# Strassen's seven products in the first product of two MLPs, with the first layer's second product over two tiles at a time

## The chip, the cores and the metric

The kernel runs on one core of a Trainium2 chip, as one program. Its time is the device time of one execution in microseconds (us); several runs are given by their median. Within a core, PE multiplies matrices, DVE and ACT work elementwise on SBUF and PSUM, POOL elementwise on SBUF alone, and SP issues the DMAs. Each engine works through a list of its own in order, and waits on semaphores for the others.

## The reference

A backbone of two layers over 256 context tokens and 512 latent tokens, 1024 features wide, in float32. The first layer has windowed attention, the second a two-way RWKV-7 scan; each is followed by the same MLP:

```python
def sq_relu_mlp(h, w1, w2):
    return jnp.square(jax.nn.relu(h @ w1)) @ w2
...
x = x + gt2 * sq_relu_mlp(rmsnorm(x, norm2_g[i]) * (1.0 + sc2) + sh2, mlp_w1[i], mlp_w2[i])
```

w1 is 1024 x 4096 and w2 4096 x 1024. The first layer's MLP runs over all 768 tokens (context with its own shift, scale and gate), the second's over the 512 latent ones. Attention and scan are not touched by the change.

## The kernel before

Activations lie transposed: a tile has 128 features on the partitions and the tokens along the free dimension, so X is 8 tiles of 128 x 768 (first layer) or 128 x 512 (second).

Every large product is made of three. A float32 value is split into `hi`, its value in the PE's faster float32 format (fp32r), and `lo`, the remainder; `mm3` (L357) then adds hi x hi, hi x lo and lo x hi into one PSUM bank, each as one matmul per 512 columns. So 768 columns take two matmuls, of 512 and of 256, for each of the three (`halves`, L372). `split` (L328) makes `hi` of a weight tile by a copy on ACT or POOL in turn and `lo` by a subtraction on DVE (L337). Activations are split the same way: `normed` (L304) multiplies X by the norm's factors (L313, tile `nu`), makes `hi` with the shift on ACT (L316) and `lo` on DVE (L317), and for every third tile on POOL (L325).

`mlp` (L664) has two steps. `w1(g)` makes four of the 32 hidden tiles: for each, `wtile` (L339) loads 128 x 1024 of w1 and splits it, `gemm` (L376) runs 8 feature tiles x `mm3`, ACT takes the relu from PSUM (L689) and its square as `hi` (L690), DVE the square again (L691) and the remainder (L692). `w2(g)` takes those four hidden tiles: for each of 8 output tiles m it loads 128 x 512 of w2 (L699), splits it (L703), runs 4 x `mm3` into a bank, and DVE adds the bank, times the gate, to X (`add_gated`, L657, two instructions of 256 and 512 columns in the first layer; L711, one, in the second). The loop calls w1(g), then w2(g-1), for 8 groups.

The framework orders the instructions of each engine: it takes what the program issues, places it by a timeline of its own estimates, and lets an instruction move ahead of others on its engine where its operands allow. `behind_norm` (L297) keeps what is issued under it behind two instructions of the norm (`norm_ins`). Buffers are handed out by pools with a number of copies per tag; an instruction that fills a copy waits for the last reader of what was in it. [...]

In front of each MLP stands its norm (`norm_stats` L263 in the first layer, the same steps at L1655 in the second): squares, sums over features by matmul, a square root on ACT, a reciprocal on DVE, a broadcast by matmul. The end of the first MLP computes the norm of the next layer the same way.

Of the kernel before, what the change touches and what calls it, by code (L numbers as in the profile page):

```python
# [166 lines left out]
HP = 0  # L167
MERGE = {True: 3, False: 1}


class K:
    def __init__(self, ctx, tc, a, stop=None, dbg=None):
# [121 lines left out]
            nc.scalar.activation(acc[:, sl], bc[:, 0:nt * P], AF.Copy)  # L294
        self.norm_ins = (act.ins, dve.ins)

    def behind_norm(self):  # L297

        st = ExitStack()
        for i in self.norm_ins:  # L300
            st.enter_context(self.tc.issue_after(i))
        return st

# [357 lines left out]
                                                ALU.mult, ALU.add)  # L661


    def mlp(self, l, bc):  # L664
# [12 lines left out]
        GF = 4
        hids = {}

        def w1(g):  # L680
            later = self.behind_norm() if g == 0 else ExitStack()
            hid = [mp.tile([P, GF, n], F32R, tag=f"hid{i}", bufs=2, name=f"hid{i}") for i in range(2)]
            for j in range(GF):
                ps = self.big("w1_ps")
# [4 lines left out]
                nc.scalar.activation(r, ps[:, 0:n], AF.Relu)  # L689
                nc.scalar.activation(hid[0][:, j], r, AF.Square)  # L690
                nc.vector.tensor_tensor(r, r, r, ALU.mult)  # L691
                nc.vector.tensor_tensor(hid[1][:, j], r, hid[0][:, j].bitcast(F32), ALU.subtract)  # L692
            hids[g] = hid

        def w2(g):
            hid = hids.pop(g)
            for m in range(8):
                raw = mp.tile([P, 512], F32, tag="w2raw", bufs=2, name="w2raw")
                nc.sync.dma_start(raw, a["w2"][l, g, m])  # L699
                wh = mp.tile([P, 512], F32R, tag="w2h", bufs=5, name="w2h")  # L700
                wl = mp.tile([P, 512], F32R, tag="w2l", bufs=5, name="w2l")
                with self.behind_norm() if g == 0 else ExitStack():
                    self.split(raw, wh, wl)  # L703
# [4 lines left out]
                if l == 0:
                    self.add_gated(ps, m, u0 + 5)
                else:  # L710
                    nc.vector.scalar_tensor_tensor(self.X[:, m], ps[:, 0:S], self.ada[:, u0 + 5, m, 0:1],  # L711
                                                   self.X[:, m], ALU.mult, ALU.add)
# [1065 lines left out]
```

## Time and profile before

| | |
|---|---|
| three runs, median (least to most) | 2259.94 us (2255.7 to 2265.13) |
| profiled execution, its own time | 2270.0 us |
| its span, first to last instruction | 2268.2 us |
| mean granted PE clock | 0.944 |
| PE busy | 2049.9 us, 90% of the span |
| DVE busy | 1320.1 us, 58% |
| ACT, POOL busy | 857.2 us, 38%; 263.7 us, 12% |
| DMA read and written | 191.80 MB and 32.60 MB |

Times are from the start of the span. A row of a timeline gives start, duration, engine, line, operation, output<-input, the shape, and in brackets how long the engine had been idle and who ended that. A grouped row gives count, busy time, mean duration in ns, and the idle time ahead of the group with its releasers. PEld is PE's loading of weights, which overlaps its matmuls. `w_ps` is the bank of either product of the MLP; `mhh` and `mhl` are hi and lo of the normed activations, `hid` those of the hidden tiles, `whi`, `wlo`, `w2h`, `w2l` those of the weights.

### The profile page before, as it was taken

The numbers are of one execution on the slowest core, as the hardware profiler recorded it, in microseconds if no ns is written. First come the engines' busy times: TensorE is split into PE (matmuls) and PEld (weight loads), VectorE is DVE, ScalarE is ACT, GpSimd is POOL, SyncE is SP. The second block draws the span as 40 slices with busy tenths as digits, with TensorE's granted clock in tenths as the row PEclk, the third lists the DMA queues.
The fourth block names the chain that finished last, engine by engine and source line by source line (L and its number), as shares of the span: only waits on it lengthen the run. The fifth ranks groups of instructions, "written<-read, shape, count | busy, mean of one in ns | idle before, by whom it ended". The sixth has DMA issues, their size and how long they took to land. (4 is left out here: it accounts for less than half of the span.)

```text
span 2268.2 us, 40460 instructions
## 1 busy us (share of the span) xinstructions
PE 2049.9 (90%) x16208; PEld 1668.3 (74%) x16208; DVE 1320.1 (58%) x2737; ACT 857.2 (38%) x1702; POOL 263.7 (12%) x362
## 2 busy tenths in 40 slices
PE   5989999979999999997979798698869887999999
PEld 4876756868888888885856687586658655787887
DVE  4465565464334343349787665888898657444443
ACT  4344454232111111116454445567647433222121
POOL 0122232010000000001010101000000101101110
PEclk9999999989999999997999898789889898999999
DMA  8344461122122121116146434113311312323322
GB/s 288 102 135 135 138 212 58 56 79 65 61 61 66 56 70 61 53 37 236 63 162 244 135 129 155 35 51 90 95 48 58 128 56 79 103 93 95 96 88 80
DMA packets 115885, 229.67 MB, mean 101 GB/s; under 512 B 12912, under 2 KB 31088, under 8 KB 115312
## 3 DMA queue, kind: packets, MB, share of 16 engines
q1 hardware_dynamic: 115696, 227.08, 31.1%
q8 instruction: 128, 2.10, 0.4%
q14 instruction: 61, 0.50, 0.1%
HBM read 191.80 MB, written 32.60 MB: 99 GB/s over the span
## 5 line engine op out<-in xcount | busy, mean ns | idle before, releaser
L337 DVE TENSOR_TENSOR wlo<-wraw,whi 128x1024 fp32r<-128x1024 f32 (+1 forms) x121 | 134.5, 1120 | 322.6 <-ACT whi L334 169.2
L364 PE MATMUL w_ps<-mhl,whi 128*128 128x512 f32 (+1 forms) x768 | 235.7, 361 | 7.3 <-DVE mhl L317 7.3
L362 PE MATMUL w_ps<-mhh,whi 128*128 128x512 f32 (+1 forms) x768 | 235.1, 361 | 7.1 <-POOL whi L336 3.4
L366 PE MATMUL w_ps<-mhh,wlo 128*128 128x512 f32 (+1 forms) x768 | 235.4, 361 | 5.0 <-DVE wlo L337 5.0
L364 PE MATMUL w_ps<-hid,w2h 128*128 128x512 f32 (+1 forms) x768 | 234.0, 359 | 0.0
L362 PE MATMUL w_ps<-hid,w2h 128*128 128x512 f32 (+1 forms) x768 | 231.4, 355 | 1.6 <-ACT mrelu L689 1.4
L366 PE MATMUL w_ps<-hid,w2l 128*128 128x512 f32 (+1 forms) x768 | 231.1, 355 | 0.0
L334 ACT ACTIVATE w2h<-w2raw 128x512 fp32r<-128x512 f32 x64 | 40.4, 631 | 330.0 <-PE w_ps L364 299.1
L660 DVE SCALAR_TENSOR_TENSOR X<-w_ps,ada,X 128x256 f32<-128x256 f32 (+1 forms) x128 | 73.1, 612 | 137.5 <-PE w_ps L366 137.5
L364 PEld LDWEIGHTS w_ps<-mhl,whi 128*128 128x128 f32 x768 | 127.7, 190 | 33.0 <-DVE mhl L317 9.8
L362 PEld LDWEIGHTS w_ps<-mhh,whi 128*128 128x128 f32 x768 | 127.8, 190 | 31.7 <-POOL whi L336 4.1
L366 PEld LDWEIGHTS w_ps<-mhh,wlo 128*128 128x128 f32 x768 | 127.8, 190 | 31.0 <-DVE wlo L337 8.0
L336 POOL TENSOR_SCALAR whi<-wraw 128x1024 fp32r<-128x1024 f32 (+1 forms) x60 | 69.2, 1154 | 673.2 <-PE w_ps L364 252.6
L366 PEld LDWEIGHTS w_ps<-hid,w2l 128*128 128x128 f32 x768 | 127.4, 189 | 23.3
L362 PEld LDWEIGHTS w_ps<-hid,w2h 128*128 128x128 f32 x768 | 125.5, 188 | 24.8 <-ACT mrelu L689 2.3
L334 ACT ACTIVATE whi<-wraw 128x1024 fp32r<-128x1024 f32 (+1 forms) x61 | 59.1, 968 | 222.7 <-PE w_ps L364 100.8
L364 PEld LDWEIGHTS w_ps<-hid,w2h 128*128 128x128 f32 x768 | 126.6, 188 | 20.7
L689 ACT ACTIVATE mrelu<-w_ps 128x768 f32<-128x768 f32 (+1 forms) x64 | 44.7, 699 | 189.6 <-PE w_ps L366 189.6
L1238 PE MATMUL g_ps<-pad,bk 128*128 128x128 f32 x640 | 98.1, 306 | 6.1 <-DVE gm L1244 2.1
L1238 PEld LDWEIGHTS g_ps<-pad,bk 128*128 128x128 f32 x640 | 86.0, 212 | 15.9 <-ACT pad L1235 7.5
L564 DVE CUSTOM_DVE_ANT_0 sm<-sc_ps,consts,vecs 128x256 f32<-128x256 f32 (+2 forms) x96 | 71.6, 760 | 40.7 <-PE pt_ps L585 21.9
L337 DVE TENSOR_TENSOR w2l<-w2raw,w2h 128x512 fp32r<-128x512 f32 x128 | 89.1, 697 | 4.8 <-ACT w2h L334 4.6
(381 smaller groups left out, 4486.1 us busy)
## 6 DMA issues: line engine op xcount, KB each, us to landing
ada_w<-ada_w SPq DMA_DIRECT2D x160, 256.0 KB, 3.5
wraw<-w SPq DMA_DIRECT2D x64, 512.0 KB, 3.2
w2raw<-w SPq DMA_DIRECT2D x128, 256.0 KB, 2.6
kt<-ada_w SPq DMA_DIRECT2D x32, 256.0 KB, 5.1
feat<-cs SPq DMA_DIRECT2D x16, 390.0 KB, 2.3
cs<-feat SPq DMA_DIRECT2D x24, 260.0 KB, 3.1
wraw<-wq SPq DMA_DIRECT2D x8, 512.0 KB, 3.8
wraw<-wo SPq DMA_DIRECT2D x8, 512.0 KB, 3.2
```

Of the source, the lines that this page charges most:

```text
L334: nc.scalar.activation(hi, raw, AF.Copy)
L336: nc.gpsimd.tensor_scalar(hi, raw, 1.0, 0.0, ALU.mult, ALU.add)
L337: nc.vector.tensor_tensor(lo, raw, hi.bitcast(F32), ALU.subtract)
L362: nc.tensor.matmul(o, wh, cut(xh, sl), start=start, stop=False)
L364: nc.tensor.matmul(o, wh, cut(xl, sl), start=False, stop=False)
L366: nc.tensor.matmul(o, wl, cut(xh, sl), start=False, stop=stop)
L564: nc.vector.tensor_tensor_reduce(sm[:, :nk], ps[:, :nk], self.c["band"][:, b0:b0 + nk], rs[:, h:h + 1], self.v["sink"][:, hd:hd + 1], ALU. ...
L660: self.nc.vector.scalar_tensor_tensor(self.X[:, m, sl], ps[:, sl], self.ada[:, u, m, s:s + 1], self.X[:, m, sl], ALU.mult, ALU.add)
L689: nc.scalar.activation(r, ps[:, 0:n], AF.Relu)
L1238: nc.tensor.matmul(g[:, P * k:P * k + P], it.BK[:, d, b + k], pv[:, :, k], start=True, stop=True)
```

## The change

The first product is computed for two hidden tiles at a time. The two tiles' weights and the activations are each cut into 2 x 2 blocks: weights by hidden tile and by half of the features (blocks of 128 x 512), activations by half of the features and half of the tokens (four tiles of 128 x H, with H 384 in the first layer and 256 in the second). Strassen's algorithm in Winograd's form needs seven block products in place of eight, and sums of blocks: four sums of activations, made once (`block_sums`), four of weights per pair, and seven additions of results. A block product is 4 feature tiles x three matmuls of H columns. The very first pair is computed plainly, from the four blocks in their original state, while the norm is still running; `block_sums` then overwrites them.

Seven split blocks of activations replace the eight tiles (`mbh`, `mbl`). In `pair`, of the seven weight remainders DVE makes four and POOL three; POOL also makes one sum of weights, and part of the block sums. ACT makes every `hi`. DVE adds the results from PSUM; relu and square become one instruction of DVE (L807). Weights of the first product are loaded into the MLP's own pool.

In the first layer GF, the number of hidden tiles that the second product sums in PSUM, goes from 4 to 2: there are 16 groups in place of 8, w2 tiles are 128 x 256, and `add_gated` runs twice as often. Every other remainder of w2 is made by POOL there. In the second layer GF stays 4.

The core of the diff:

```diff
+    def normed_w(self, u2, x, bc, gain, sh, l, n, bh, bl):
...
+        for k in range(NF):
+            u = u2[k % 4][:, k // 4]
+            hi, lo = ((t[:, 0:7:6, k % 4] if k < 4 else t[:, 1:3, k % 4]) for t in (bh, bl))
+            uh = u.rearrange("p (a h) -> p a h", a=2)
+            for s, t0, w in streams:
+                c = slice(t0, t0 + w)
+
+                with self.tc.issue_after(done[k - 2]) if k > 1 else ExitStack():
+                    nc.vector.scalar_tensor_tensor(u[:, c], x[k][:, c], gain[:, k, s:s + 1], bc[:, c], ALU.mult, ALU.mult)
+                if l == 0:
+                    nc.scalar.activation(u[:, c], u[:, c], AF.Identity, bias=sh[:, k, s:s + 1])
+            if l == 0:
+                act = nc.scalar.activation(hi, uh, AF.Copy)
+                dve = nc.vector.tensor_tensor(lo, uh, hi.bitcast(F32), ALU.subtract)
...
+    def block_sums(self, u2, H, bh, bl):
...
+        for k in range(4):
+            u0a, u0b, u1a, u1b = (u2[k][:, i, h * H:h * H + H] for i in range(2) for h in range(2))
+            nc.vector.tensor_tensor(u0b, u0b, u0a, ALU.subtract)
+            nc.vector.tensor_tensor(u1b, u1b, u0b, ALU.subtract)
+            ts.append((u1b, u0b, u0a, u1a))
+        for b, i in ((4, 0), (3, 1), (5, 2), (6, 3)):
+            for k in range(4):
+                t = ts[k][i]
+                if b == 5:
+                    nc.gpsimd.tensor_tensor(t, ts[k][0], t, ALU.subtract)
+                if b == 6:
+                    nc.gpsimd.tensor_tensor(t, t, ts[k][0], ALU.subtract)
+                act = nc.scalar.activation(bh[:, b, k], t, AF.Copy)
+                eng = nc.gpsimd if b == 6 else nc.vector
+                lo = eng.tensor_tensor(bl[:, b, k], t, bh[:, b, k].bitcast(F32), ALU.subtract)
...
     def mlp(self, l, bc):
...
+        n = T if l == 0 else S
+        H = n // 2
+        GF = 2 if l == 0 else 4
...
+        def first_pair():
...
+            for k in range(NF):
+                q = ((0, 6), (1, 2))[k // 4]
+                for ps, (wh, wl) in zip(banks, ws):
+                    for w, t, e in ((wh, bh, 0), (wh, bl, 1), (wl, bh, 2)):
+                        for h in range(2):
+                            nc.tensor.matmul(ps[:, 512 * h:512 * h + H], w[:, k * P:k * P + P], t[:, q[h], k % 4],
+                                             start=(k == 0 and e == 0), stop=(k == NF - 1 and e == 2))
+            with self.behind_norm():
+                self.block_sums(u2, H, bh, bl)
...
+        def pair(m, hid, j):
...
+            def product(tag, raw, b, eng=None):
+                bank = self.ps.tile([P, 512], F32, tag=tag, bufs=2 if tag == "t" else 1, name="w1p_ps")[:, 0:H]
+                wh, wl = block()
+                nc.scalar.activation(wh, raw, AF.Copy)
+                (eng or nc.vector).tensor_tensor(wl, raw, wh.bitcast(F32), ALU.subtract)
+                for k in range(4):
+                    self.mm3([(bank, slice(0, H))], wh[:, k * P:k * P + P], wl[:, k * P:k * P + P],
+                             bh[:, b, k], bl[:, b, k], k == 0, k == 3)
+                return bank
...
+            def square(i):
+                nc.vector.scalar_tensor_tensor(c[i], c[i], 0.0, c[i], ALU.max, ALU.mult)
+                nc.scalar.activation(hid[0][:, j + i], c[i], AF.Copy)
+                nc.vector.tensor_tensor(hid[1][:, j + i], c[i], hid[0][:, j + i].bitcast(F32), ALU.subtract)
+
+            nc.vector.tensor_tensor(s1, a21, a22, ALU.add)
+            nc.vector.tensor_tensor(s2, s1, a11, ALU.subtract)
+            nc.vector.tensor_tensor(s4, a12, s2, ALU.subtract)
+            nc.gpsimd.tensor_tensor(a21, a11, a21, ALU.subtract)
+            b, p1 = product("a", a11, 0), keep()
+            nc.scalar.activation(p1, b, AF.Copy)
+            add(c11, product("t", a12, 1, nc.gpsimd), p1)
+            p3 = product("t", s4, 2)
+            q = add(keep(), product("o", s2, 4), p1)
+            p5 = product("a", s1, 3)
+            w = add(keep(), p5, q)
+            add(c12, p3, w)
+            square(0)
+            z = add(keep(), product("t", a21, 5, nc.gpsimd), q)
+            add(c22, p5, z)
+            add(c21, product("o", a22, 6, nc.gpsimd), z)
+            square(1)
...
+        def w2(g):
...
+            W = P * GF
+            c0 = W * g % 512
+            for m in range(8):
+                raw = mp.tile([P, W], F32, tag="w2raw", bufs=2, name="w2raw")
...
+                with self.behind_norm(self.sums_ins) if g == 0 else ExitStack():
+                    nc.scalar.activation(wh, raw, AF.Copy)
+                    eng = nc.gpsimd if l == 0 and m % 2 else nc.vector
+                    eng.tensor_tensor(wl, raw, wh.bitcast(F32), ALU.subtract)
```

`keep` and the sums have buffers of their own; `add` is one DVE addition of a bank and a kept tile. The split weights rotate in four half tiles in the first layer and six in the second.

More of the change, by code (lines that the diff above doesn't have):

```diff
@@ L168 @@
 MERGE = {True: 3, False: 1}
+WL = (0, 1)
+NSQ = 3
+NRW = (2, 3)
 class K:
@@ new lines, in mlp, with block, keep, add @@
+    def mlp(self, l, bc):
+        if l not in WL:
+            return self.mlp_plain(l, bc)
+        nc, a = self.nc, self.a
+        st = ExitStack()
+        mp = st.enter_context(self.tc.tile_pool(reuse_waits=RW.get("mlp", "pool"), name=f"mlp{l}", bufs=1))
+        g2 = self.norm_gain(2, l, f"g2_{l}")
+        u0 = 6 * l
+        n = T if l == 0 else S
+        H = n // 2
+        GF = 2 if l == 0 else 4
+        bh = mp.tile([P, 7, 4, H], F32R, name="mbh")
+        bl = mp.tile([P, 7, 4, H], F32R, name="mbl")
+        Xk = [self.X[:, k] for k in range(NF)]
+        u2 = [mp.tile([P, GF, n], F32, tag=f"hid{k % 2}", bufs=2, name="nu")[:, 0:2] for k in range(4)]
+        self.normed_w(u2, Xk, bc, g2, self.ada[:, u0 + 3], l, n, bh, bl)
+        parts = self.halves if l == 0 else lambda ps: [(ps[:, 0:S], slice(0, S))]
+        hids = {}
+        turn = {"i": 0}
+        def block():
+            if l:
+                return [mp.tile([P, 512], F32R, tag=f"sw{i}", bufs=6, name=("swh", "swl")[i]) for i in range(2)]
+            h = turn["i"] % 2
+            if h == 0:
+                turn["w"] = [self.wp.tile([P, 1024], F32R, tag=t, name=t) for t in ("whi", "wlo")]
+            turn["i"] += 1
+            return [w[:, 512 * h:512 * h + 512] for w in turn["w"]]
+        def first_pair():
+            banks, ws = [self.big("w1_ps") for _ in range(2)], []
+            for j in range(2):
+                raw = mp.tile([P, 1024], F32, tag="w1raw", bufs=NRW[l], name="w1raw")
+                nc.sync.dma_start(raw, a["w1"][l, j])
+                ws.append([self.wp.tile([P, 1024], F32R, tag=t, name=t) for t in ("whi", "wlo")])
+                self.split(raw, *ws[j], eng=1)
+            for k in range(NF):
+                q = ((0, 6), (1, 2))[k // 4]
[6 more added lines that the diff above has]
+                self.block_sums(u2, H, bh, bl)
+            hid = hid_pair()
+            for j, ps in enumerate(banks):
+                r = mp.tile([P, n], F32, tag="sq", bufs=NSQ, name="mrelu")
+                nc.scalar.activation(r.rearrange("p (a h) -> p a h", a=2),
+                                     ps.rearrange("p (a c) -> p a c", a=2)[:, :, 0:H], AF.Relu)
+                nc.scalar.activation(hid[0][:, j], r, AF.Square)
+                nc.vector.tensor_tensor(r, r, r, ALU.mult)
+                nc.vector.tensor_tensor(hid[1][:, j], r, hid[0][:, j].bitcast(F32), ALU.subtract)
+            return hid
+        def pair(m, hid, j):
+            raws = []
+            for i in range(2):
+                raw = mp.tile([P, 1024], F32, tag="w1raw", bufs=NRW[l], name="w1raw")
+                nc.sync.dma_start(raw, a["w1"][l, m + i])
+                raws.append(raw)
+            a11, a12, a21, a22 = (raws[i][:, 512 * h:512 * h + 512] for i in range(2) for h in range(2))
+            s1, s2, s4 = (mp.tile([P, 512], F32, tag="sums", bufs=3, name="wsum") for _ in range(3))
+            def product(tag, raw, b, eng=None):
[7 more added lines that the diff above has]
+                return bank
+            def keep():
+                return mp.tile([P, H], F32, tag="keep", bufs=4, name="keep")
+            def add(o, bank, t):
+                nc.vector.tensor_tensor(o, bank, t, ALU.add)
+                return o
+            c = [mp.tile([P, n], F32, tag="sq", bufs=NSQ, name="mrelu") for _ in range(2)]
+            c11, c12, c21, c22 = (c[i][:, h * H:h * H + H] for i in range(2) for h in range(2))
+            def square(i):
[19 more added lines that the diff above has]
+            square(1)
+        def hid_pair():
+            return [mp.tile([P, GF, n], F32R, tag=f"hid{i}", bufs=2, name=f"hid{i}") for i in range(2)]
+        def w1(g):
+            hid = first_pair() if g == 0 else hid_pair()
+            for j in range(0, GF, 2):
+                if g or j:
+                    with self.behind_norm() if GF * g + j == 2 else ExitStack():
+                        pair(GF * g + j, hid, j)
+            hids[g] = hid
+        def w2(g):
+            hid = hids.pop(g)
+            W = P * GF
+            c0 = W * g % 512
+            for m in range(8):
+                raw = mp.tile([P, W], F32, tag="w2raw", bufs=2, name="w2raw")
+                nc.sync.dma_start(raw, a["w2"][l, W * g // 512, m, :, c0:c0 + W])
+                wh = mp.tile([P, W], F32R, tag="w2h", bufs=5, name="w2h")
+                wl = mp.tile([P, W], F32R, tag="w2l", bufs=5, name="w2l")
+                with self.behind_norm(self.sums_ins) if g == 0 else ExitStack():
+                    nc.scalar.activation(wh, raw, AF.Copy)
+                    eng = nc.gpsimd if l == 0 and m % 2 else nc.vector
+                    eng.tensor_tensor(wl, raw, wh.bitcast(F32), ALU.subtract)
+                ps = self.big("w2_ps")
+                for k in range(GF):
+                    self.mm3(parts(ps), wh[:, k * P:k * P + P], wl[:, k * P:k * P + P],
+                             hid[0][:, k], hid[1][:, k], k == 0, k == GF - 1)
+                if l == 0:
+                    self.add_gated(ps, m, u0 + 5)
+                else:
+                    nc.vector.scalar_tensor_tensor(self.X[:, m], ps[:, 0:S], self.ada[:, u0 + 5, m, 0:1],
+                                                   self.X[:, m], ALU.mult, ALU.add)
+        NG = FF // P // GF
+        for g in range(NG + 1):
+            if g < NG:
+                w1(g)
+            if g > 0:
+                w2(g - 1)
+        if l == 0:
+            self.next_bc = self.norm_stats(mp, self.xp2, Xk, 0, T, "sq", NSQ)
+        st.close()
@@ L665, in mlp, with mlp_plain @@
+    def mlp_plain(self, l, bc):
         nc, a = self.nc, self.a
```

19 lines of the change are left out of this document (17 added, 2 removed).

## The prediction

> **What bounds the kernel now.** I read the page's busy times first, then the two MLPs cut by time, then the pace of their matmuls. Page, first lines:
>
> ```profile
> span 2268.2 us, 40460 instructions
> PE 2049.9 (90%) x16208; PEld 1668.3 (74%) x16208; DVE 1320.1 (58%) x2737; ACT 857.2 (38%) x1702; POOL 263.7 (12%) x362
> ```
>
> Busy time by stretch, us and (instructions): start and body of the first MLP, start and body of the second:
>
> ```profile
> 465.00:490.00 25.00, 15.95 (x71) 12.70 (x70) 24.16 (x35) 13.66 (x24) 8.04 (x4) 0.77 0.24 85
> 490.00:1021.00 531.00, 530.29 (x3008) 460.52 (x3006) 212.78 (x289) 92.74 (x117) 34.62 (x45) 1.00 0.19 60
> 1892.00:1915.00 23.00, 15.21 (x48) 10.16 (x48) 18.64 (x21) 8.86 (x14) 7.68 (x7) 0.76 0.35 117
> 1915.00:2263.00 348.00, 344.34 (x1489) 278.50 (x1488) 161.19 (x216) 71.88 (x109) 34.22 (x44) 1.00 0.29 92
> ```
>
> The columns are PE, PEld, DVE, ACT, POOL, granted clock, DMA. In both bodies PE never rests and DVE is busy 40 and 46%: there a matmul that goes is time that goes, as long as the added vector work keeps up. In both starts DVE is the busy one. How fast matmuls follow each other, PE alone by stretch: first MLP (512 and 256 columns in turn), second MLP in its first product, second MLP in its second:
>
> ```profile
> 560.00:960.00 400.00, 400.00 (x2266) 1.00 0.20 61
> 2198.00:2218.00 20.00, 20.00 (x88) 1.00 0.13 40
> 2230.00:2260.00 30.00, 30.00 (x134) 1.00 0.32 108
> ```
>
> So 400/2266 = 0.1765 us a matmul, 0.353 for 768 columns. A row counts two that only reach in: 20/86 = 0.2326 and 30/132 = 0.2273 for 512. For 256 columns with other weights each time, the attention's value product, 29 steps between these two:
>
> ```profile
> 83.78 0.28 PE L499 MATMUL v_ps<-wv,hh 128*128 128x256 f32 x1
> ...
> 87.22 0.28 PE L501 MATMUL v_ps<-wv,hl 128*128 128x256 f32 x1
> ```
>
> 3.44/29 = 0.1186. No row has 384; midway between 0.1186 and 0.2273 is 0.173, half of 0.353 is 0.1765: I take 0.175.
>
> **The matmuls.** Two output tiles took 2 x 8 x 3 = 48 products over all columns; a pair now takes 7 x 4 x 3 = 84 over half of them. First MLP: 48 x 0.353 = 16.94, now 84 x 0.175 = 14.70; 15 pairs, **-33.7** (-36 to -32). Second: 48 x 0.2326 = 11.16, now 84 x 0.1186 = 9.96; 15 pairs, **-18.0**. The first pair stays plain, in halves (96 matmuls): +0.1 for both. The second product keeps its matmuls. Sum **-51.6**.
>
> **What DVE gets.** Rows by form, first MLP, then second (busy us, mean ns | idle before):
>
> ```profile
> L660 DVE SCALAR_TENSOR_TENSOR X<-w_ps,ada,X 128x512 f32<-128x512 f32 x64 | 47.4, 741 | 0.0
> L337 DVE TENSOR_TENSOR w2l<-w2raw,w2h 128x512 fp32r<-128x512 f32 x64 | 43.5, 681 | 0.2 <-ACT w2h L334 0.2
> L692 DVE TENSOR_TENSOR hid<-mrelu,hid 128x768 fp32r<-128x768 f32 x32 | 31.4, 981 | 1.1
> L660 DVE SCALAR_TENSOR_TENSOR X<-w_ps,ada,X 128x256 f32<-128x256 f32 x64 | 30.9, 483 | 137.5 <-PE w_ps L366 137.5
> L691 DVE TENSOR_TENSOR mrelu<-mrelu 128x768 f32<-128x768 f32 x32 | 30.6, 955 | 11.9 <-ACT hid L690 11.9
> ```
>
> ```profile
> L690 ACT ACTIVATE hid<-mrelu 128x768 fp32r<-128x768 f32 x32 | 27.1, 847 | 1.0
> ...
> L334 ACT ACTIVATE w2h<-w2raw 128x512 fp32r<-128x512 f32 x32 | 20.2, 632 | 220.1 <-PE w_ps L364 211.8 <-DMA w2raw<-w 8.3
> ```
>
> ```profile
> L711 DVE SCALAR_TENSOR_TENSOR X<-w_ps,ada,X 128x512 f32<-128x512 f32 x64 | 47.9, 749 | 67.4 <-PE w_ps L366 67.4
> L337 DVE TENSOR_TENSOR w2l<-w2raw,w2h 128x512 fp32r<-128x512 f32 x64 | 45.6, 712 | 4.6 <-ACT w2h L334 4.4
> L692 DVE TENSOR_TENSOR hid<-mrelu,hid 128x512 fp32r<-128x512 f32 x32 | 22.0, 690 | 0.9
> L691 DVE TENSOR_TENSOR mrelu<-mrelu 128x512 f32<-128x512 f32 x32 | 22.0, 689 | 12.8 <-ACT hid L690 12.8
> ```
>
> From SBUF, 128 columns cost 0.13 (0.955 against 0.689 for 256 more): 0.56 for 384, 0.42 for 256. From PSUM 384 costs 0.61, between 0.741 and 0.483. DVE per pair, first MLP: three sums of weights and four remainders, 7 x 0.68; seven adds from PSUM, 7 x 0.61; squares, 2 x (0.955 + 0.981); then a second product over two tiles: four remainders x 0.42 and eight times both adds to X, 8 x 1.224 (twice as often as now): 4.8 + 4.3 + 3.9 + 1.7 + 9.8 = 24.4, beside PE's 14.70 + 48 x 0.353 = 31.6. Second MLP: 7 x 0.69 + 7 x 0.483 + 4 x 0.69 + 4 x (0.712 + 0.749) = 16.8, beside 9.96 + 48 x 0.2273 = 20.9. ACT copies seven half tiles x 0.63, one bank, two hidden tiles x 0.85 and eight small w2 tiles x 0.4, 10 of 31.6, and 9 of 20.9 in the second: nothing. The bytes loaded are the same; the first load of the next stage (wkv) now stands ahead of the MLP's in SP's queue, into free buffers: nothing either.
>
> POOL takes subtractions of two tiles. Its rows, and what DVE did beside one of them:
>
> ```profile
> L325 POOL TENSOR_TENSOR mhl<-nu,mhh x4: 1277/1873/3603, 472.9 to 1905.4; 128x768 fp32r<-128x768 f32 x2, 128x512 fp32r<-128x512 f32 x2
> ```
>
> ```profile
> 1905.39 1.28 POOL L325 TENSOR_TENSOR mhl<-nu,mhh 128x512 fp32r<-128x512 f32 x1 [1.65 <-ACT mhh L324]
> ```
>
> ```profile
> 1905.46 2.29 DVE L337 TENSOR_TENSOR wlo<-wraw,whi 128x1024 fp32r<-128x1024 f32 x1
> ```
>
> A POOL subtraction of 512 is 1.28, so 4 x 1.28 + 4 x 0.64 = 7.7 a pair in the first MLP and 5.1 in the second. The DVE subtraction of 1024 that began 0.07 behind one took 2.29; by 0.68 for 512 and 0.13 per 128 it should take 1.20, so it lost 1.09, nearly the rest of POOL's. DVE's work of that kind (two tiles in SBUF) is 10.3 of its 24.4 and 10.4 of its 16.8, so I charge four and six tenths of POOL's time: 24.4 + 3.1 = 27.5 of 31.6, and 16.8 + 3.1 = 19.9 of 20.9. In between PE has both products to choose from. First MLP, PE, the turn from first to second product (w_ps<-hid is the second), before:
>
> ```order
> L364 MATMUL w_ps<-mhl,whi 128x512
> L364 MATMUL w_ps<-mhl,whi 128x256
> L366 MATMUL w_ps<-mhh,wlo 128x512
> L366 MATMUL w_ps<-mhh,wlo 128x256
> L362 MATMUL w_ps<-hid_4831,w2h 128x512
> L362 MATMUL w_ps<-hid_4831,w2h 128x256
> ```
>
> and now, in the middle of one half-block product (w1p_ps):
>
> ```order
> L366 MATMUL w1p_ps<-mbh,whi 128x384
> L368 MATMUL w1p_ps<-mbl,whi 128x384
> L370 MATMUL w1p_ps<-mbh,wlo 128x384
> L366 MATMUL w_ps<-hid_6249,w2h 128x512
> L366 MATMUL w_ps<-hid_6249,w2h 128x256
> ```
>
> Whole phases have become alternation, two second-product tiles inside a product, so most waits for DVE have cover. I take 0.2 us lost a pair in the first MLP and 0.4 in the second (0 to 0.5 and 1.0, DVE and POOL laid end to end): **+9**.
>
> **The starts.** DVE rows: the first of the norm in each MLP, an add of the next norm, the last add to X:
>
> ```profile
> 465.68 0.75 DVE L313 SCALAR_TENSOR_TENSOR nu<-X,g,nacc 128x512 f32<-128x512 f32 x1 [2.65 <-ACT nacc L294]
> 1018.20 0.96 DVE L272 TENSOR_TENSOR nacc<-nacc,nsq 128x768 f32<-128x768 f32 x1 [0.97 <-ACT nsq L271]
> 1020.32 1.14 DVE L660 SCALAR_TENSOR_TENSOR X<-w_ps,ada,X 128x256 f32<-128x256 f32 x2 [1.16 <-PE w_ps L366]
> 1891.99 0.75 DVE L313 SCALAR_TENSOR_TENSOR nu<-X,g,nacc 128x512 f32<-128x512 f32 x1 [2.16 <-ACT nacc L294]
> 2263.05 0.75 DVE L711 SCALAR_TENSOR_TENSOR X<-w_ps,ada,X 128x512 f32<-128x512 f32 x1 [1.97 <-PE w_ps L366]
> ```
>
> The first MLP's first load into its own buffers, and the first relu of the second:
>
> ```profile
> 458.73 0.33 SPq L699 DMA_DIRECT2D w2raw<-w  x1
> ```
>
> ```profile
> 1914.64 0.60 ACT L689 ACTIVATE mrelu<-w_ps 128x512 f32<-128x512 f32 x1 [8.72 <-PE w_ps L366]
> ```
>
> First MLP: 555.8 for 1536 x 0.353 = 542.2 of matmuls, 13.6 lost; second: 371.8 for 768 x (0.2326 + 0.2273) = 353.2, 18.6 lost. After the change the first w1 tiles also come into the MLP's own buffers, so not before 458.73 (in the kernel before they are loaded ahead), and ACT's split of them stands in front of the norm's square root, which with the whole norm queues behind that load: 2 lost. DVE then needs 0.483 + 0.741 + 0.981 = 2.2 a feature tile, some 22 with lead for eight, for 16.8 of matmuls: 5. Behind it stands the new list. DVE, first MLP, behind the norm, before:
>
> ```order
> L691 TENSOR_TENSOR mrelu<-mrelu 128x768
> L692 TENSOR_TENSOR hid_4832<-mrelu,hid_4831 128x768
> L337 TENSOR_TENSOR wlo<-wraw,whi 128x1024 x2
> L691 TENSOR_TENSOR mrelu<-mrelu 128x768
> L692 TENSOR_TENSOR hid_4832<-mrelu,hid_4831 128x768
> ```
>
> and now (L704, L705, L716 are the sums of blocks, L811 and L812 sums of weights, L789 the remainder that the second pair's first product waits for):
>
> ```order
> L704 TENSOR_TENSOR nu<-nu 128x384 x4
> L811 TENSOR_TENSOR wsum<-w1raw 128x512
> L705 TENSOR_TENSOR nu<-nu 128x384 x2
> L716 TENSOR_TENSOR mbl<-nu,mbh 128x384
> L705 TENSOR_TENSOR nu<-nu 128x384
> L716 TENSOR_TENSOR mbl<-nu,mbh 128x384
> L705 TENSOR_TENSOR nu<-nu 128x384
> L716 TENSOR_TENSOR mbl<-nu,mbh 128x384 x2
> L812 TENSOR_TENSOR wsum<-wsum,w1raw 128x512
> L789 TENSOR_TENSOR wlo<-w1raw,whi 128x512
> ```
>
> What stood there was squares and remainders of whole tiles; now the sums of blocks come ahead of the remainder that PE needs next. Up to the second pair's first square DVE has 20 x 0.56, ten subtractions of 512 x 0.68, three of 256 x 0.42, the first pair's squares 3.9, six adds x 0.61 and one square 1.9: 29 us, beside the second pair and 36 matmuls of the second product, 21: 8 lost. POOL has 12 x 0.96 + 4 x 1.28 + 2 x 0.64 = 18 in the same stretch, half on DVE's account: 9. Sum 2 + 5 + 8 + 9 = 24, +10.6 on 13.6. Second MLP: the first two tiles ended at 1914.64, 22.6 behind the first nu; now DVE needs 16 x 0.75 + 2 x 1.2, some 15.5 with lead, for 11.4 of matmuls: 4. Its list is 20 x 0.42, 18 x 0.69, 5 x 0.71, squares 2.8 and 2.8, seven adds x 0.483, 33 beside 25 (two pairs and 24 matmuls): 8. POOL 12 x 0.64 + 9 x 1.28 = 19, by half 9.6. Sum 22, +3.1 on 18.6. Starts **+14** (-6 if POOL costs DVE nothing and the lists overlap, +32 if all of it).
>
> [...] In both starts the granted clock was 0.77 and 0.76, in the bodies 1.00. [...]
>
> **The end.** The first MLP's last group is half as long (17 us), and the next norm's squares are added in it: 8 x (1.22 + 0.96 + 0.2) = 19: **+2**. The rest of the program stands in nearly the same order: 0, give or take 3.
>
> **Sum.** -51.6 + 9 + 14 + 2 = -27. The profiled execution took 2270.0, 10 above the median 2259.94; on its scale 2243, on the median's **2233**.
>
> **Rivals.**
> - Nothing lost in alternation or starts: DVE's order leaves PE a second product at nearly every turn, and POOL's work may fall into DVE's pauses. -52 + 2: 2210.
> - DVE and POOL end to end: starts +32, bodies 15 x 0.5 + 15 x 1.0 = +22, end +2: -52 + 56, 2265, no change. For it: the 2.29. Against: 14 and 6 us of DVE's work a pair are adds from PSUM, and all 64 of these lay between 736 and 751 ns, whatever POOL did:
>
> ```profile
> L711 DVE SCALAR_TENSOR_TENSOR X<-w_ps,ada,X x64: 736/750/751, 1954.8 to 2263.0; 128x512 f32<-128x512 f32 x64
> ```
>
> - Slower: the same, and DVE, working in order, also waits for ACT's copy ahead of each remainder. It decides from 0.25 us a pair (30 pairs, 7 us) on; at 0.5 us, 2280. Its 0.2 and 4.6 us of waiting for ACT before 128 remainders speak against it.
> - The halves bring no speed, because a weight load bounds a short matmul:
>
> ```profile
> L362 PEld LDWEIGHTS w_ps<-mhh,whi 128*128 128x128 f32 x768 | 127.8, 190 | 31.7 <-POOL whi L336 4.1 <-ACT mhh L316 3.5 <-ACT whi L334 1.0
> ```
>
> At 0.190 a matmul the second MLP's pair takes 15.96: +72, the first's saves 15; with the rest some 2340. The steps of 0.1186 speak against it.
>
> **Chances.** Forecast 0.50 (2222 to 2246), nothing lost 0.22, end to end 0.16, slower 0.09, weight loads 0.01, others 0.02. Half a per cent, 11.3 us, is what a measurement of this kernel can tell from no change. Faster: 0.50 + 0.22 + 0.03 of the third = 0.75; slower 0.09 + 0.01 = 0.10; same 0.15. The range takes in the unhindered case with -36 for its price, and the nearer half of the third: 2205 to 2256.
>
> **What would show it.** Right: steps of 0.173 to 0.177 in the half products of the first MLP and 0.119 in the second; the first MLP some 538 us from its first nu to its last X, the second some 363; PE idle behind the first pair, released by DVE's or POOL's remainders; POOL subtractions over 1.28 and DVE ones over 0.69 where they meet. Wrong: PE waiting for DVE throughout a body, a clock below 1.00 there, or steps near 0.19.

## The result, and the profile after

The changed kernel took 2228.77 us (median of 4 runs, 2226.51 to 2234.92), the kernel before 2262.53 beside it (4 runs): a ratio of 0.9852, 95% interval 0.9828 to 0.9875. That is faster by 1.5%, 33.8 us; the forecast was 2233 (2205 to 2256). The profiled execution of the changed kernel took 2226.51. One of the four executions of the kernel called "starts without POOL" below, the profiled one, ran at a granted clock of 0.73 and took 2528.4 us, so its time below is the median of the other three and its stages are not in the table.

The page of the changed kernel, first lines:

```profile
span 2224.5 us, 42844 instructions
PE 1999.1 (90%) x16616; PEld 1690.3 (76%) x16616; DVE 1597.0 (72%) x3263; ACT 992.5 (45%) x2026; POOL 441.1 (20%) x470
```

PE has 51 us less to do, DVE 277 more and POOL 177 more. The ends of the two MLPs, from the DVE's timeline (start, duration; first step of the norm, last add to X, of each MLP):

```profile
460.44 1.41 DVE L682 SCALAR_TENSOR_TENSOR nu<-X,g,nacc 128x512 f32<-128x512 f32 x2 [1.53 <-ACT nacc L298]
...
985.83 1.14 DVE L664 SCALAR_TENSOR_TENSOR X<-w_ps,ada,X 128x256 f32<-128x256 f32 x2
...
1853.13 1.41 DVE L682 SCALAR_TENSOR_TENSOR nu<-X,g,nacc 128x512 f32<-128x512 f32 x2 [1.42 <-ACT nacc L298]
...
2220.19 0.75 DVE L860 SCALAR_TENSOR_TENSOR X<-w_ps,ada,X 128x512 f32<-128x512 f32 x1 [1.97 <-PE w_ps L370]
```

The first MLP takes 526.5 us where it took 555.8 (-29.3), the second 367.8 where it took 371.8 (-4.0). Together that is 33.3, nearly all of the 33.8 of the medians. (The two spans differ by 43.7; the other 10 lie in parts that the change leaves alone. Their lengths wander: over twelve profiles of this study the first MLP begins between 459.5 and 466.7 us, and 861 to 871 us lie between the MLPs.)

The pace of the matmuls, from the PE's timeline (x2 is a pair of 512 and 256 columns): 29 steps of 384 columns, then 36 pairs of the second product, then 14 steps of 256 columns in the second MLP:

```profile
947.12 0.34 PE L366 MATMUL w1p_ps<-mbh,whi 128*128 128x384 f32 x1
...
952.16 0.34 PE L370 MATMUL w1p_ps<-mbh,wlo 128*128 128x384 f32 x1
952.34 0.52 PE L366 MATMUL w_ps<-hid,w2h 128*128 128x512 f32 x2
...
964.83 0.51 PE L366 MATMUL w_ps<-hid,w2h 128*128 128x512 f32 x2
...
1886.37 0.28 PE L366 MATMUL w1p_ps<-mbh,swh 128*128 128x256 f32 x1
...
1888.04 0.40 PE L370 MATMUL w1p_ps<-mbh,swl 128*128 128x256 f32 x2
```

5.04/29 = 0.1738, 12.49/36 = 0.347 (0.353 before) and 1.67/14 = 0.1193. At this pace the first MLP's 15 x 84 + 96 = 1356 half steps and 768 pairs are 502.1 us of matmuls, the second's 1356 x 0.1193 + 768 x 0.2273 = 336.3. What a stage takes beyond that I call its loss, here and below: 24.4 and 31.5 us, where it was 13.6 and 18.6. Busy time by stretch shows where the loss sits: start and body of the first MLP, then of the second:

```profile
460.40:530.00 69.60, 55.42 (x275) 51.40 (x274) 64.06 (x87) 39.54 (x73) 36.93 (x23) 0.86 0.14 46
530.00:987.00 457.00, 455.79 (x2621) 422.64 (x2620) 337.37 (x558) 138.33 (x260) 125.73 (x114) 1.00 0.20 65
1853.00:1923.00 70.00, 51.91 (x329) 48.14 (x330) 68.64 (x94) 38.57 (x73) 34.08 (x25) 0.81 0.30 104
1923.00:2180.00 257.00, 255.49 (x1621) 231.57 (x1620) 201.10 (x320) 97.93 (x169) 67.16 (x47) 1.00 0.30 93
```

In the bodies PE rests 1.2 us of 457 (the end included) and 1.5 of 257, at a clock of 1.00, with DVE busy 74 and 78%. In the starts it rests 14 and 18 us, and DVE works nearly all the time. What PE waited for (us in total, times, longest), in the first start and then, the three longest, in the second:

```profile
PE w1p_ps L366 <- ACT whi L788: 4.8, 1, 4.8
PE w_ps L762 <- ACT mbh L686: 3.6, 1, 3.6
PE w1p_ps L370 <- DVE wlo L789: 3.0, 2, 1.5
PE w1p_ps L366 <- DVE mrelu L799: 1.4, 1, 1.4
PE w1p_ps L370 <- POOL wlo L789: 1.3, 2, 0.9
```

```profile
PE w1p_ps L366 <- ACT swh L788: 9.4, 1, 9.4
PE w1p_ps L366 <- DVE keep L799: 4.6, 1, 4.6
PE w_ps L762 <- ACT mbh L689: 3.1, 1, 3.1
```

The longest wait of each is named after ACT, but ACT only copies a sum that DVE had just finished. How the 4.8 us came about, from the timeline of all engines:

```profile
481.16 7.27 POOL L814 TENSOR_TENSOR w1raw<-w1raw 128x512 f32<-128x512 f32 x1 [45.52 <-DVE wsum L811]
488.40 0.98 POOL L711 TENSOR_TENSOR nu<-nu 128x384 f32<-128x384 f32 x1
489.42 1.48 ACT L714 ACTIVATE mbh<-nu 128x384 fp32r<-128x384 f32 x3 [2.96 <-POOL nu L711]
489.97 0.79 DVE L716 TENSOR_TENSOR mbl<-nu,mbh 128x384 fp32r<-128x384 f32 x1 [2.68 <-ACT mbh L714]
490.69 1.48 DVE L813 TENSOR_TENSOR wsum<-w1raw,wsum 128x512 f32<-128x512 f32 x1
492.07 0.61 ACT L788 ACTIVATE whi<-wsum 128x512 fp32r<-128x512 f32 x1
492.74 0.69 PE L366 MATMUL w1p_ps<-mbh,whi 128*128 128x384 f32 x1 [4.77 <-ACT whi L788]
```

A POOL subtraction of 512 columns, 1.28 us by itself, took 7.27: DVE went from one step with two inputs in SBUF to the next for 6.1 us of it, and POOL's step ended 1.1 us after DVE came to rest. POOL's sums of blocks came that much later, ACT's copy of one behind them, and DVE, which works in order, stood 2.68 us before the remainder of that copy. Behind it in DVE's list was the sum (L813) that PE's next product needed, and that step took 1.48 us for 0.68, with a POOL subtraction of 384 columns (1.31 us) beside it. So steps grew in both directions, 7.27 for 1.28 on POOL and 1.48 for 0.68 on DVE. In the second start the same goes on without DVE ever resting; the sum (L813) for which PE waited 9.4 us stood behind these six remainders, which take 0.41 us each in the kernel without POOL:

```profile
1876.02 5.25 DVE L716 TENSOR_TENSOR mbl<-nu,mbh 128x256 fp32r<-128x256 f32 x6
1881.20 1.20 DVE L813 TENSOR_TENSOR wsum<-w1raw,wsum 128x512 f32<-128x512 f32 x1
```

### The profile page after: what moved, and what is told of

It is laid out like the page before. It is cut to its first block, busy times and chain, and to the rows that moved or that the text cites. A ratio compares the mean times of both kernels' runs of the same rounds, so it can differ in the third digit from the quotient of the medians.

```text
span 2224.5 us, 42844 instructions
## 1 busy us (share of the span) xinstructions
PE 1999.1 (90%) x16616; PEld 1690.3 (76%) x16616; DVE 1597.0 (72%) x3263; ACT 992.5 (45%) x2026; POOL 441.1 (20%) x470
## 5 line engine op out<-in xcount | busy, mean ns | idle before, releaser
L850 ACT ACTIVATE w2h<-w2raw 128x256 fp32r<-128x256 f32 (+1 forms) x192 | 92.9, 487 | 287.0 <-PE w_ps L368 259.7
L664 DVE SCALAR_TENSOR_TENSOR X<-w_ps,ada,X 128x256 f32<-128x256 f32 (+1 forms) x256 | 145.2, 610 | 101.0 <-PE w_ps L370 100.6
L366 PE MATMUL w1p_ps<-mbh,whi 128*128 128x384 f32 x420 | 142.4, 341 | 6.2 <-ACT whi L788 4.8
L370 PE MATMUL w1p_ps<-mbh,wlo 128*128 128x384 f32 x420 | 142.8, 341 | 4.4 <-DVE wlo L789 3.0
L368 PE MATMUL w1p_ps<-mbl,whi 128*128 128x384 f32 x420 | 142.4, 339 | 0.0
L366 PE MATMUL w1p_ps<-mbh,swh 128*128 128x256 f32 x420 | 120.7, 288 | 15.5 <-ACT swh L788 9.4
L368 PE MATMUL w1p_ps<-mbl,swh 128*128 128x256 f32 x420 | 119.9, 286 | 0.3 <-DVE mbl L716 0.3
L370 PE MATMUL w1p_ps<-mbh,swl 128*128 128x256 f32 x420 | 118.7, 285 | 0.0
L366 PEld LDWEIGHTS w1p_ps<-mbh,swh 128*128 128x128 f32 x420 | 81.4, 194 | 19.0 <-ACT swh L788 9.6
L1447 PEld LDWEIGHTS g_ps<-pad,bk 128*128 128x128 f32 x640 | 83.4, 205 | 13.4 <-ACT pad L1444 7.2
L341 DVE TENSOR_TENSOR wlo<-wraw,whi 128x1024 fp32r<-128x1024 f32 (+1 forms) x57 | 55.1, 983 | 52.7 <-ACT whi L338 32.9
```

The lines of the kernel that those rows point to most:

```text
L341: nc.vector.tensor_tensor(lo, raw, hi.bitcast(F32), ALU.subtract)
L366: nc.tensor.matmul(o, wh, cut(xh, sl), start=start, stop=False)
L368: nc.tensor.matmul(o, wh, cut(xl, sl), start=False, stop=False)
L370: nc.tensor.matmul(o, wl, cut(xh, sl), start=False, stop=stop)
L664: self.nc.vector.scalar_tensor_tensor(self.X[:, m, sl], ps[:, sl], self.ada[:, u, m, s:s + 1], self.X[:, m, sl], ALU.mult, ALU.add)
L850: nc.scalar.activation(wh, raw, AF.Copy)
```

## The experiments

Theory A, formed on the profile: each MLP's gain is its own, PE's time is the measure in the bodies, and what is lost in the starts (and, with more POOL work, in the second body) comes from POOL and DVE holding each other up in steps on SBUF (7.27 us for 1.28, 1.48 for 0.68). The rivals: the gain comes from elsewhere; the two engines work side by side and only DVE's list counts; the half clock is what the starts lose. The table has each kernel's time (a median; the kernels ran on several chips, so compare them by the ratio), its ratio to the kernel before on the same chip, and the length of the two MLPs with the loss in brackets (a stage in the old form against 542.2 or 353.2 us of matmuls). In the code cuts below, remarks behind # and in brackets are not part of the code.

| kernel | us | ratio, 95% interval | first MLP | second MLP |
|---|---|---|---|---|
| before | 2262.5 | 1 | 555.8 (13.6) | 371.8 (18.6) |
| changed | 2228.8 | 0.9852, 0.9828 to 0.9875 | 526.5 (24.4) | 367.8 (31.5) |
| only the first MLP changed | 2231.6 | 0.9853, 0.9832 to 0.9875 | 526.2 (24.1) | old form, 367.2 (14.0) |
| only the second changed | 2261.8 | 0.9995, 0.9981 to 1.0009 | old form, 556.8 (14.6) | 366.3 (30.0) |
| starts without POOL | 2215.6 | 0.9799, 0.9768 to 0.9831 | - | - |
| bodies without POOL | 2226.6 | 0.9827, 0.9803 to 0.9851 | 527.9 (25.8) | 363.3 (27.0) |
| no POOL in either | 2206.2 | 0.9739, 0.9715 to 0.9763 | 519.1 (17.0) | 354.1 (17.8) |
| the same, second MLP in the old form | 2217.2 | 0.9799, 0.9774 to 0.9824 | 519.1 (17.0) | old form, 366.6 (13.4) |
| idle matmuls in the starts | 2224.1 | 0.9834, 0.9805 to 0.9864 | 524.8 | 364.6 |
| four more steps a pair on POOL | 2267.6 | 1.0017, 1.0005 to 1.0028 | 530.6 (28.5) | 405.3 (69.0) |
| four more steps a pair on DVE | 2243.8 | 0.9906, 0.9879 to 0.9934 | 530.2 (28.1) | 379.5 (43.2) |
| no POOL, sums of weights first | 2214.5 | 0.9776, 0.9753 to 0.9800 | 519.2 (17.1) | 355.6 (19.3) |
| no POOL, no sums of blocks (other outputs) | 2192.0 | 0.9680, 0.9655 to 0.9705 | 511.7 (9.6) | 344.7 (8.4) |

**One MLP at a time.**

```
-WL = (0, 1)
+WL = (0,)      # only the first;  (1,) only the second
```

> Only the first MLP in the new form, the second as before. Theory A (each MLP's gain is its own: fewer matmul steps in a body where PE never waits, less the waits of its start): the first MLP's share as the profiles show it, -29 us, so some 2233 us; the prediction's own terms for this stage (-33.7 matmuls, +10.6 start, +3 body, +2 end) give -18, 2244. Theory B (the gain comes from elsewhere: order of loads, other stages, clock): nothing near -29, or the second MLP's change is needed for it.

> Only the second MLP in the new form, the first as before. Theory A: -4 us, the second MLP's share as the profiles show it (367.8 against 371.8), so about 2258, no difference that can be told; the prediction's own terms (-18 matmuls, +3 start, +6 body) give -9, 2253. Theory B: with the first MLP plain, SP's and POOL's queues reach the second one as before and it gains its -18 in full, 2244.

The first MLP alone gives the whole gain, 0.9853 against 0.9852, and the second alone gives nothing that can be told, 0.9995. Theory A. That the second MLP in the old form took 367.2 in one profile and 371.8 in another shows how much such a length wanders; its new form is worth 0 to 4 us, and not the 16.9 of its matmuls.

**POOL out of the starts, out of the bodies.**

```
 (block_sums, both starts)
-                    nc.gpsimd.tensor_tensor(t, ts[k][0], t, ALU.subtract)
+                    nc.vector.tensor_tensor(t, ts[k][0], t, ALU.subtract)
...
-                eng = nc.gpsimd if b == 6 else nc.vector
+                eng = nc.vector
 (pair; for the bodies the two engines here are exchanged)
+            pool = nc.vector if m == 2 else nc.gpsimd
-            nc.gpsimd.tensor_tensor(a21, a11, a21, ALU.subtract)
+            pool.tensor_tensor(a21, a11, a21, ALU.subtract)
 (and pool for nc.gpsimd in products 2, 6 and 7, and in w2's split of the first group;
  for the bodies, of all other groups, and block_sums stays as it was)
```

> In both starts (sums of blocks, second pair, first turn of the second product) POOL's sums and remainders go to DVE; the bodies keep theirs. Theory A, the two engines exclude each other when both read SBUF: POOL's 18 us (first) and 19 us (second) become 10 and 11 on DVE, and DVE's own pieces fall from 1.24 to 1.49 us back to 0.55 and 0.68; both starts 0 to 8 us shorter, 2215 to 2228 against 2229 for the changed kernel. Theory B, the two work side by side and DVE's list is what the PE waits for: 10 and 11 us more on that list, 2240 to 2250.

> The bodies of both MLPs without POOL (its four remainders and a sum of each pair and half of the small second-product remainders go to DVE), the starts keep it. Theory A (exclusion; DVE alone carries 24.4 + 4.4 of 31.6 us a pair in the first MLP and 16.8 + 2.8 of 20.9 in the second): no waits in the first body, 0 to 0.3 us a pair in the second, 2229 to 2234. Theory B (side by side, POOL is what keeps DVE off the path): DVE at 91 and 94% makes the PE wait 0.5 us a pair or more, 2244 and up.

With POOL out of the starts the kernel is shorter: 0.9799 against 0.9852, some 12 us, the better end of A's range and the opposite of B, though the two intervals just touch. The bodies without POOL: 0.9827, not told apart from the changed kernel's 0.9852, its 2226.6 just under A's range, and the second MLP 4.5 us shorter in the profile, no more than such a length wanders; B's 2244 did not come, although DVE then carries all of it.

**No POOL at all, and what the second MLP is then worth.** The two edits above together; and the same with the second MLP in the old form.

> Both MLPs in the new form and none of their added work on POOL: starts and bodies together. Theory A (POOL and DVE exclude each other, POOL's work costs the start more than it saves DVE): the start's 13 us and the second body's 4 us add, 2211 to 2217, and the PE's losses in the first 70 us of each MLP fall from 18 and 23 us to under 10. Theory B (DVE at 91 and 94% of the bodies without POOL makes the PE wait): the two do not add, 2222 to 2235.

> The first MLP in the new form without POOL, the second as before. It tells whether the second MLP's new form is worth anything once its start is free of POOL. Theory A: the second MLP gains its -16 of matmuls less some 6 us of start, so this kernel is 8 to 13 us slower than the one with both and no POOL: 2221 to 2228. Theory B (the second MLP's start eats the gain whatever engine does the sums): the same time as that one within 4 us.

2206.2 us, 0.9739 (0.9715 to 0.9763): better than A's best end, and the fastest kernel here that computes everything. Against the kernel whose bodies alone are without POOL (0.9827) only the starts differ, and here the intervals are well apart: the first MLP falls from 527.9 to 519.1 us, the second from 363.3 to 354.1. This is the clearest evidence that POOL's part costs the starts time. Now the second MLP's new form is worth something: without it the ratio is 0.9799, and the intervals do not meet; 366.6 becomes 354.1, -12.5. (With the second MLP in the old form the kernel is 11 us slower, within A's 8 to 13; its 2217 itself lies 4 below A's range.) The page of the kernel without POOL:

```profile
span 2203.6 us, 42676 instructions
PE 1998.1 (91%) x16616; PEld 1690.3 (77%) x16616; DVE 1616.4 (73%) x3471; ACT 993.8 (45%) x2026; POOL 180.6 (8%) x262
```

DVE took over 208 instructions on which POOL had been busy 260 us, and is busy 19 us more. What it had saved by handing these steps over it had lost again in its own, which took longer beside POOL's. One can see it on single groups, changed kernel first (busy us, mean ns of one):

```profile
L789 DVE TENSOR_TENSOR swl<-wsum,swh 128x512 fp32r<-128x512 f32 x45 | 39.6, 883 | 0.7 <-ACT swh L788 0.7
L789 DVE TENSOR_TENSOR wlo<-wsum,whi 128x512 fp32r<-128x512 f32 x45 | 35.0, 802 | 0.0
L812 DVE TENSOR_TENSOR wsum<-wsum,w1raw 128x512 f32<-128x512 f32 x30 | 29.9, 996 | 0.1
L664 DVE SCALAR_TENSOR_TENSOR X<-w_ps,ada,X 128x512 f32<-128x512 f32 x128 | 94.7, 740 | 0.0
```

and without POOL:

```profile
L790 DVE TENSOR_TENSOR swl<-wsum,swh 128x512 fp32r<-128x512 f32 x45 | 30.4, 682 | 0.8 <-ACT swh L789 0.5
L790 DVE TENSOR_TENSOR wlo<-wsum,whi 128x512 fp32r<-128x512 f32 x45 | 29.6, 683 | 6.4 <-ACT whi L789 6.4
L813 DVE TENSOR_TENSOR wsum<-wsum,w1raw 128x512 f32<-128x512 f32 x30 | 20.4, 681 | 0.0
L664 DVE SCALAR_TENSOR_TENSOR X<-w_ps,ada,X 128x512 f32<-128x512 f32 x128 | 94.8, 741 | 0.0
```

Steps with both inputs in SBUF fall from 0.80 to 1.00 us to the 0.68 of a step alone; the add that has one input in PSUM stays at 0.74. The starts and bodies again, without POOL:

```profile
463.60:533.00 69.40, 61.69 (x317) 58.22 (x317) 65.94 (x120) 40.62 (x75) 0.00 (x0) 0.89 0.18 57
533.00:983.00 450.00, 448.51 (x2578) 415.90 (x2576) 361.99 (x662) 136.70 (x259) 0.00 (x0) 1.00 0.20 64
1846.00:1916.00 70.00, 60.73 (x394) 56.35 (x395) 69.51 (x136) 40.69 (x78) 0.00 (x0) 0.89 0.32 109
1916.00:2160.00 244.00, 244.00 (x1560) 222.43 (x1559) 195.62 (x352) 95.26 (x162) 0.00 (x0) 1.00 0.29 92
```

PE now rests 8 and 9 us in the starts (14 and 18 before this edit). The first body's DVE is busy 80% and lets PE rest as little as before; the second's PE never rests.

**The half clock.** Idle matmuls keep PE at work where it waited for the third product of the second pair; their results are overwritten.

```
+                for _ in range(warm):        # (26, 72)[l] for the third product of pair 2, else 0
+                    nc.tensor.matmul(bank, bh[:, 0, 0, 0:P], bh[:, 0, 0], start=True, stop=True)
                 wh, wl = block()
```

> The changed kernel with idle matmuls (26 of 384 columns, 72 of 256, into a bank that the next product overwrites) ahead of the second pair's third product, so that the PE does not rest there for 4.8 and 9.4 us. Theory A (the half clock behind these rests is lost time): the half-clock windows behind them go, 3 to 6 us less, 2223 to 2226. Theory B (what the PE waits for there comes from DVE and POOL, and a slower PE only waits less afterwards): 2229 within 3 us, or slower by what the idle matmuls push back.

The clock behind the long waits, changed kernel (PE, PEld, DVE, ACT, POOL, then the granted clock):

```profile
490.30:500.50 10.20, 6.89 (x20) 6.39 (x21) 10.12 (x9) 5.75 (x13) 10.20 (x9) 0.50 0.15 51
1876.10:1886.30 10.20, 3.18 (x13) 3.07 (x14) 10.04 (x16) 4.70 (x10) 7.35 (x8) 0.50 0.16 53
1893.10:1900.00 6.90, 3.67 (x15) 3.48 (x16) 6.90 (x14) 3.36 (x6) 0.16 (x1) 0.51 0.42 152
```

and, with idle matmuls, the stretch in the first start that answers to the first of these:

```profile
494.30:504.50 10.20, 6.84 (x23) 6.42 (x23) 10.16 (x10) 6.05 (x14) 10.20 (x8) 0.67 0.14 51
```

In those windows matmuls of 384 columns follow each other in 0.32 us (0.174 at full clock) and of 256 in 0.213 (0.119), so nearly half of the PE time inside them is lost, some 3 us in each MLP. The idle matmuls left a clock of 0.67 in the first window in place of 0.50, so it became shorter and did not go, and the MLPs became 1.7 and 3.2 us shorter; the time, 0.9834, cannot be told from the changed kernel's 0.9852. The direction is A's; it is not shown.

**More work on one engine or the other.** Four more subtractions of 512 columns in each pair from the third on, on POOL in one kernel and on DVE in the other. The results go unused.

```
+            if m > 2:
+                for _ in range(4):
+                    e = mp.tile([P, 512], F32, tag="extra", bufs=1, name="extra")
+                    nc.gpsimd.tensor_tensor(e, a11, a12, ALU.subtract)     # or nc.vector
```

> The changed kernel with four more subtractions of 512 columns on POOL in each pair from the third on (28 pairs, 5.1 us each at 1.28), results unused. Theory A (exclusion): first body 23.4 + 2 of 31.6 us, no waits; second body, 10.4 of DVE's two-SBUF work and 10.2 of POOL's exclude each other and DVE has 6 more from PSUM, 26 of 20.9: 2 to 5 us a pair, so 2255 to 2300, all of it in the second MLP. Theory B (side by side): POOL is 40 and 50% busy and costs nothing: 2229 to 2233.

> The changed kernel with four more subtractions of 512 columns on DVE, not POOL, in each pair from the third on (28 pairs, results unused); with the same four on POOL it took 38 us longer. Theory A (what counts is time in which one of the two holds SBUF, and DVE does such a subtraction in 0.68 where POOL takes 1.28): 2.7 us a pair, 26 of 31.6 us in the first body and 19 of 20.9 in the second, 0 to 0.3 us a pair lost there: 2229 to 2236. Theory B (DVE's own list is what the second body hangs on): 28 x 2.7 or at least 14 x 2.7 us more, 2260 and up.

On POOL they cost 38.8 us over the changed kernel, and the second MLP has 37.5 of it: its body cannot hold them, the first one's can. That is A's pattern and size. Of the 37.5, PE's rest in the second body makes up 17 and its rest in the second start 7; in 24 us of that body the clock was halved as well (0.96 over all of it), which by the steps above is up to 11. Bodies of the two MLPs with the work on POOL, then with it on DVE:

```profile
532.00:992.00 460.00, 459.14 (x2639) 425.54 (x2637) 372.06 (x562) 140.47 (x265) 210.94 (x165) 1.00 0.20 64
1927.00:2222.00 295.00, 276.62 (x1678) 247.67 (x1677) 240.86 (x332) 102.20 (x176) 144.54 (x97) 0.96 0.26 84
```

```profile
533.00:993.00 460.00, 459.10 (x2634) 425.63 (x2632) 376.29 (x615) 137.72 (x262) 134.25 (x115) 1.00 0.21 65
1933.00:2202.00 269.00, 263.65 (x1649) 237.54 (x1648) 242.75 (x374) 98.07 (x172) 71.69 (x49) 0.99 0.30 91
```

In the second body with the work on POOL neither engine is full (DVE 82%, POOL 49%), and yet PE rests 18 us. Laid over each other, one of the two is at work in 263 of the 295 us, and DVE is at work in all of the 18; DVE's steps with two SBUF inputs took up to 1.2 us for 0.68. So the pair is taken for 89% of the body, though neither engine is. On DVE the same steps cost 15.0 us: 8 above A's upper end, 16 below B's lower one. They hold DVE at 90% there, at 0.92 us each with POOL's own work still beside them:

```profile
L818 DVE TENSOR_TENSOR extra<-w1raw 128x512 f32<-128x512 f32 x46 | 42.2, 918 | 3.1 <-DMA w1raw<-w 2.9
```

I had counted them at 0.68. PE rests 5.4 us in this body, 3.9 more than in the changed kernel's. Of the other 11, the trace shows 2 as longer rest in the second start, and in each MLP some 7 us more at half clock (the mean clock of the profiled execution was 0.937, against 0.939), which by the steps above is 3 us of PE's time each; the last 3 are not explained.

**What is left of the starts, without POOL.** First the sums of weights put ahead of the sums of blocks, then the sums of blocks left out.

```
             with self.behind_norm():
+                ready[2] = prep(2)          # pair 2: loads, s1, s2, s4, a11 - a21
                 self.block_sums(u2, H, bh, bl)
```

> The kernel without POOL, and in both starts the second pair's sums of weights are put ahead of the sums of blocks. Theory A (the PE's waits of 2.9 and 6.2 us for the third product's weights come from their place in DVE's list): these go, 2197 to 2203 against 2206. Theory B (the list as a whole is too long and the next thing in it is late instead): 2204 to 2209.

```
 (block_sums)
+        self.sums_ins = self.norm_ins
+        return
 (product)
+                b = (0, 1, 2, 2, 1, 1, 0)[b]
```

> The kernel without POOL and without the sums of blocks: products 4 to 7 read unsummed blocks, so the outputs differ; the matmuls, the sums of weights and all else stay. It leaves out 32 DVE steps a start, 17 us in the first MLP and 13 in the second. Theory A (what is left of the starts' loss, some 8 and 14 us, is this list): 2192 to 2199. Theory B (it is the first weights, ACT or the half clock): 2203 to 2209.

The new order is no faster: 0.9776 against 0.9739, with MLPs of nearly the same length. Its 2214.5 lies above both ranges; on this chip the kernel before took 2266.6, some 3 us more than beside the kernel without POOL, and most of the rest lies outside the MLPs. PE's waits in the first start, before this edit (without POOL) and after it:

```profile
PE w1p_ps L366 <- ACT whi L789: 2.9, 1, 2.9
```

```profile
PE w1p_ps L366 <- ACT mbh L714: 2.1, 1, 2.1
PE w1p_ps L370 <- DVE wlo L799: 1.8, 2, 0.9
```

The wait for the weights went and one for the sums of blocks came, as B said: the list is too long, whatever stands first in it. Left out altogether, the sums of blocks give 2192.0, in A's range; the losses fall to 9.6 and 8.4 us, below those of the kernel before. So in the kernel without POOL the sums of blocks, with ACT's copies of them, cost the starts 7.4 and 9.4 us, for 17 and 13 us of DVE's time.

## Why the prediction was right, and where its terms were off

- **Matmuls: right.** It said 0.175 for 384 columns and 0.1186 for 256; measured 0.1738 and 0.1193. First MLP -33.7 said; the half products gave 15 x (16.94 - 14.60) = -35.1. Second -18.0 said, -16.9 measured. One term it did not have: the second product's pair of 512 and 256 columns fell from 0.353 to 0.347 us, 768 times, -4.7. Why is open; nothing here was tried on it. No run has the seven products without the second product's change to two tiles, so this split of the first MLP's gain rests on the two paces.
- **Bodies: said +9, measured next to nothing.** PE rests 1.2 and 1.5 us in them (before 0.7 and 3.7, over somewhat longer stretches). That alternation of products would cover the waits for DVE was said in the prediction, but it still charged 0.2 and 0.4 us a pair; the term should have been near 0, as its first rival had it.
- **Starts: said +14; with the ends they have nearly all of the measured +23.7.** The first MLP's loss grew by 10.8, where start and end together were said to add 12.6. The second's grew by 12.9, and 3.1 were said for its start: this is the term that was mis-sized, by some 10 us. Two things are missing in it. POOL's 19 us were charged to DVE by half. In the second start of the kernel whose bodies are free of POOL, POOL has 12 x 0.64 + 4 x 1.28 = 12.8 us to do; by half that is 6.4, less than the 12 x 0.41 + 4 x 0.68 = 7.6 that DVE takes for the same steps, so by this charge the start would have grown when DVE took them over. The second MLP became 9.2 us shorter: POOL's time counted in full, which gives 5.2, and by an estimate some 3 us of PE's time at half clock that went with it (the mean clock of the profiled executions was 0.937, then 0.941, some 20 us less of half clock over the whole execution). And the half clock, for which the sum has no term, was there in the changed kernel: some 3 us of PE's time in each MLP by the windows at 0.50 and 0.51. The lower bound given for the starts, -6, does not follow from the terms: without POOL's 18.6 the +14 is -5, and without the lists' 8 and 8 as well it is -21.
- **End: said +2, measured 0.** The 1.2 us for which PE rests in the first MLP's body include its last group.
- **The sum.** Said -51.6 + 9 + 14 + 2 = -27. Measured -57.0 of matmuls and +23.7 of loss, -33.3. The two errors in the losses, 9 too much in the bodies and about as much too little in the second start, cancel: that 25 of loss were said and 23.7 came is luck, while the matmul term was right by its mechanism. The rest is mostly the second product's pace.
- **The rivals.** That nothing would be lost (2210) did not come by itself; without POOL it did, at 2206. DVE and POOL end to end (2265) was wrong for the bodies as changed, where PE rested 1.2 and 1.5 us; with four more POOL steps a pair the time was 2267.6. DVE's wait of 2.68 us for ACT was part of one wait, the 4.8 us in the first start; in the bodies PE hardly rests, so it decided nothing there. Weight loads bound nothing: steps of 0.1193.
- **What the prediction did not ask** is whether POOL's part was worth having. It took the split between the engines as given and priced it as a cost, with the row in hand (2.29 us for a step of 1.20) from which the answer follows: if a step of one waits for a step of the other, 1.28 us on POOL cannot relieve 0.68 on DVE.

## What to carry to other kernels

Where the steps of two engines grow beside each other, as here (7.27 us for 1.28, 1.48 for 0.68), moving a step from one to the other relieves the first only if the second does it in less time, or while the first is at work that does not clash (the adds from PSUM took 0.74 with POOL's part and without it); here POOL's 260 us of help were worth 19 to DVE and cost the kernel some 22. When matmuls are taken out of a body in which PE never rests, and the added vector work fits, the gain is theirs in full, so look at the start for what eats it: the sums that such an algorithm needs once come at the moment when nothing else is there for PE to do. And when a wait is named after ACT or DVE, follow its list back to the first step that waited for someone else.

## What the runs showed of the hardware that was not expected

- A POOL subtraction of 512 columns, 1.28 us alone, took 7.27 us while 13 DVE steps went by; in five profiles of this study (the changed kernel, only the first MLP changed, idle matmuls, more work on POOL, more on DVE) the same step took 7.27 to 7.29. In the second start of the changed kernel DVE did not rest either, and yet POOL's steps of 256 columns took only 0.85 to 1.17 there (an estimate from the 1.28 is 0.64 alone), while DVE's of 0.41 took 0.87. What decides whether POOL gets its turn is open.
- With more work on POOL, PE rested 18 us of the 295 of a body in which DVE was busy 82% and POOL 49%, with DVE at work in all of these 18 us.
- Taking 208 steps over from POOL made DVE's busy time grow by 19 us, 0.09 us a step of 0.4 to 0.7.
- The second product's step pair became 1.7% faster in the kernel that sums two tiles in place of four at a time, cause unknown.
